# Splitting three raw weight blocks ahead of the first sum in the seven-product pairs of a float32 encoder

## The chip, the core and the metric

The kernel runs on one NeuronCore of a Trainium2 chip. The metric is the device time of one execution in microseconds. The reported time is the median of three runs; one further execution was profiled, and its span runs from the first to the last instruction of the program.

The engines are named as the profile names them: PE is TensorE (matmuls), PEld its weight loads, DVE is VectorE, ACT is ScalarE, POOL is GpSimd and SP is SyncE, which here issues the weight DMAs. Every engine works through its own queue strictly in order.

## The reference

The reference is a two-layer encoder trunk in float32, with 256 tokens of width 2048. Each layer has a token mixer (a chunked spatial gate in layer 0, grouped-query attention in layer 1), a cross-attention into 256 memory tokens, and a dense SwiGLU feed-forward block:

```python
def swiglu(h, w_gate_up, w_down):
    gate, up = jnp.split(h @ w_gate_up, 2, axis=-1)
    return (jax.nn.silu(gate) * up) @ w_down

for l in range(DEPTH):                      # 2
    h = rms_norm(x, g_mix[l])
    ...                                     # token mixer, memory attention
    x = x + jnp.concatenate([tok_out, mem_out], axis=-1) @ w_out[l]
    x = x + swiglu(rms_norm(x, g_ffn[l]), w_gate_up[l], w_down[l])
```

`w_gate_up` is 2048 x 11264 and `w_down` 5632 x 2048 for each layer. The change touches the feed-forward block alone.

## The kernel before

**Three matmuls for one.** Every float32 operand is split in two: a high part `hi`, its copy in the rounded type fp32r, and a low part `lo`, the operand less its high part. A float32 product is then three fp32r matmuls (`matmul3`, lines 198 to 200): L198 is weight-high times activation-high, L199 weight-high times activation-low, L200 weight-low times activation-high. So L198 and L199 need only `whi`, the high part of the weights, and L200 needs `wlo`. The splits of weights are made on chip: ACT makes `whi` by a copy (L254), and DVE makes `wlo` by a subtraction (L255).

**Units.** The feed-forward block works in pairs of 512 output columns (class `Pair`): a gate and an up block of the same 512 features, or two column blocks of `w_down`. A pair goes through its rows in 8 units (6 in the last third of `w_down`); a unit is 256 rows, two DMAs of 512 KB into one tile `raw` with four blocks of 128x512. In the tile's order they are called w01, w00, w10 and w11. There are four `raw` buffers, so the DMA of a unit can start when the unit four places earlier has no reader left.

**Eights and sevens.** An ordinary unit, an eight, makes eight block products (`eight`, 24 matmuls of 512 columns): one split of all four blocks serves them. Some units make seven products instead, after Winograd's form of Strassen's algorithm (`seven`, 21 matmuls). They need four sums of weight blocks. `prepare` makes them on DVE: t1 = w01 + w00 in place of w01 in the `raw` tile (L347, called the first sum below), and t2, t3 and t4 in a tile `T` (L348 to L350). `prepare` of the next unit is called ahead of the products of the present one. There are 82 sevens: three in each gate/up pair (two in the first pair of a layer), standing as first, third and fifth unit, and 18 in the down pairs.

**Split tiles.** `halves` writes one `whi` and one `wlo` tile. An eight takes one such pair of tiles. A seven takes two: its first holds t1, w00, w10 and w11 (one ACT copy and one DVE subtraction of 128x2048), its second t2, t3 and t4 (128x1536 each). There are three buffers of either kind, so a copy into a split tile starts when PE has made its last matmul with the split tile three places earlier.

**Products and banks.** Products 1, 5, 6 and 7 add up in banks of the tag `m`, products 2, 3, 4 and 8 in banks of the tag `acc`. Product 1 uses w00, 2 uses w10, 3 uses w11; 5, 6, 7 and 4 use t1, t2, t3 and t4. In the first unit of a pair 1, 5, 6 and 7 are written ahead of 2, 3 and 4; in later sevens 1, 2 and 3 stand first.

**Order.** The order in each engine's queue isn't the order of the code. The framework's scheduler sets it when the program is built, by its own estimate of what is ready. It places single matmuls of different units, and DVE's sums, subtractions and bank sums, among one another.

Of the kernel before, what the change touches and what calls it, by code (L numbers as in the profile page):

```python
# [10 lines left out]
F32 = mybir.dt.float32  # L11
F32R = mybir.dt.float32r
AF = mybir.ActivationFunctionType
ALU = mybir.AluOpType
AX = mybir.AxisListType

P = 128
# [10 lines left out]
NB = 512  # L28
# [3 lines left out]
KC4 = 4  # L32
# [4 lines left out]
KC3 = 3  # L37


class Parts:  # L40
# [8 lines left out]
    def get(self, kc, t):  # L49
        return self.ap[kc, t]  # L50
# [3 lines left out]
def encoder(ctx: ExitStack, tc: tile.TileContext, x, mem, g_mix, g_ffn, w_in_a, g_v_a, w_spatial, b_spatial,  # L54
            w_in_b, g_q_b, g_k_b, g_mem, w_mem_kv, g_mq, g_mk, w_out, w_gate_up, w_down, rope_c, rope_s, out):
    nc = tc.nc
# [4 lines left out]
    wp = ctx.enter_context(tc.tile_pool(name="wp", bufs=W_TILES))  # L61
# [9 lines left out]
    def nm(s):  # L71
        uid[0] += 1
        return f"{s}_{uid[0]}"
# [25 lines left out]
    def tick():  # L99
        clock[0] += 1  # L100
        run_due(clock[0])
# [146 lines left out]
    def halves(raw, n, step=KC4):  # L248

        hi = wp.tile([P, KC4, NB], F32R, tag="whi", name=nm("whi"))[:, :n]  # L250
        lo = wp.tile([P, KC4, NB], F32R, tag="wlo", name=nm("wlo"))[:, :n]
        for c in range(0, n, step):
            cut = slice(c, min(c + step, n))
            nc.scalar.copy(hi[:, cut], raw[:, cut])  # L254
            nc.vector.tensor_tensor(lo[:, cut], raw[:, cut], hi[:, cut].bitcast(F32), ALU.subtract)  # L255
        return [(hi[:, c, :], lo[:, c, :]) for c in range(n)]

    class Linear:


# [49 lines left out]
    class Pair:  # L310
# [54 lines left out]
            matmul3(self.bank[name], a, b, self.part[name] == 1, self.part[name] == self.of.get(name, self.most))  # L365

        def seven(self, i, raw, T):
            t1, w00, w10, w11 = halves(raw, KC4)
            t2, t3, t4 = halves(T, KC3)
            get, (q5, s2, q7, q3) = self.parts.get, self.sums[i]  # L370
            k0, k1 = 2 * i, 2 * i + 1
            inner = [(1, get(k0, 0), w00), (5, q5, t1), (6, s2, t2), (7, q7, t3)]
            outer = [(2, get(k1, 0), w10), (3, q3, w11), (4, get(k1, 1), t4)]
            if self.bank:
                inner, outer = inner[:1] + outer[:2], inner[1:] + outer[2:]
            for some in (inner, outer):
                for name, a, b in some:
                    self.add(name, a, b)
                tick()
# [225 lines left out]
    for l in range(DEPTH):  # L605
# [105 lines left out]
        else:  # L711
# [12 lines left out]
            for c in range(3):  # L724
                acc = linear(hT, w, c * NB)
                attend(head_norm(acc, norm.r, ghead["q"], True), (7, 8, 11, 13), lambda: own["k"], lambda: own["v"],
                       lambda h, c=c: (4 * c + h) // 3, 4 * c, cat)
# [32 lines left out]
        for chunk in (range(0, 4), range(4, 8), range(8, 11)):  # L760
# [20 lines left out]
            for f, g in pairs.items():  # L781
                g.run(pairs.get(f + 1))
                for t in range(NT):
                    a = kp.tile([P, NB], F32, tag="sg", name=nm("sg"), bufs=2)
# [63 lines left out]
```

## Time and profile before

| | |
|---|---|
| median of 3 runs | 2045.56 us (2045.43 to 2046.12) |
| profiled execution, its own time | 2045.77 us |
| its span, first to last instruction | 2044.0 us |
| PE busy | 2028.7 us, 99% of the span |
| DVE busy | 1604.7 us, 79% |
| ACT busy | 1095.1 us, 54% |
| feed-forward block of layer 0 | about 339 to 1029 us of the span |
| feed-forward block of layer 1 | about 1355 to 2040 us |

A row of a group names the line, the engine, the operation, what is written and read, the shapes and the count; then the busy time and the mean duration in ns; then the engine's idle time ahead of these instructions and what ended it. A row of a timeline gives start, duration, engine, line, operation and tiles; idle time ahead of it stands in brackets. Consecutive 512-column matmuls start 0.227 us apart while PE is supplied, and each is shown as 0.39 us long because they overlap.

### The profile page before, as it was taken

What the parts mean: (1) busy time and instruction counts of PE and PEld (TensorE: products, weight loads), DVE (VectorE), ACT (ScalarE), POOL (GpSimd) and SP (SyncE); (2) the same over time, 40 slices, a digit from 0 to 9 for tenths busy, and PEclk for the clock granted to TensorE, in tenths of its full rate; (3) what the DMA queues carried; (4) which work ended last, traced back from release to release, by engine and by line L of the source; (5) the groups of instructions that cost most, each with busy time, mean ns of one, the idle gap of its engine ahead of it and who ended that gap; (6) DMA issues with size and microseconds to landing.
All of it is one profiled execution on the core that took longest, in us unless ns stands there. A gap on an engine that the chain in (4) does not pass through costs nothing.

```text
span 2044.0 us, 24691 instructions
## 1 busy us (share of the span) xinstructions
PE 2028.7 (99%) x9298; PEld 1679.5 (82%) x9298; DVE 1604.7 (79%) x1862; ACT 1095.1 (54%) x1389; POOL 49.1 (2%) x80
## 2 busy tenths in 40 slices
PE   8999999999999999999999999999999999999999
PEld 6888888888888888888888888888888888888887
DVE  5575557998888988887666876589979899798976
ACT  7765455455444554445556665555544455444552
POOL 2010000000000000000010100000000000000000
PEclk9999999999999999999999999999999999999999
DMA  9754554655656556566556434655666555665554
GB/s 330 249 177 159 187 187 148 227 168 203 208 190 220 169 201 208 200 215 209 188 190 212 157 124 142 206 179 172 205 206 211 200 176 195 206 216 196 181 197 138
DMA packets 202432, 396.08 MB, mean 194 GB/s; under 512 B 11068, under 2 KB 11432, under 8 KB 202312
## 3 DMA queue, kind: packets, MB, share of 16 engines
q1 hardware_dynamic: 198800, 385.79, 56.4%
q0 software_dynamic: 2048, 6.42, 1.0%
q10 hardware_dynamic: 1464, 2.28, 0.3%
q8 instruction: 73, 1.20, 0.2%
q14 instruction: 47, 0.39, 0.1%
HBM read 390.26 MB, written 4.19 MB: 193 GB/s over the span
## 4 chain that ended last, share of the span: by engine, by line
PE 94%; DVE 3%; DMA 1%; issue 1%; ACT 1%; SPq 0%; DVEq 0%; ACTq 0%
PE acc L200 27%; PE acc L198 27%; PE acc L199 27%; PE m L200 4%; PE m L198 4%; PE m L199 4%; PE m L204 2%; DVE wlo L255 1%; DMA raw<-in_w_gate_up 1%; ACT whi L254 0%; PE m L500 0%; DMA x<-in_x 0%; DMA raw<-in_w_down 0%; PE m L643 0%; DVE x L413 0%
## 5 line engine op out<-in xcount | busy, mean ns | idle before, releaser
L255 DVE TENSOR_TENSOR wlo<-raw,whi 128x2048 fp32r<-128x2048 f32 (+2 forms) x465 | 836.4, 1822 | 227.0 <-ACT whi L254 224.8
L254 ACT CAST whi<-raw 128x2048 fp32r<-128x2048 f32 (+2 forms) x465 | 700.9, 1539 | 584.6 <-PE acc L199 513.3
L198 PE MATMUL acc<-whi,h 128*128 128x512 f32 x1440 | 563.6, 392 | 0.8 <-ACT whi L254 0.8
L199 PE MATMUL acc<-whi,h 128*128 128x512 f32 x1440 | 562.6, 391 | 0.0
L200 PE MATMUL acc<-wlo,h 128*128 128x512 f32 x1440 | 523.8, 392 | 1.1 <-DVE wlo L255 1.1
L198 PE MATMUL acc<-whi,a 128*128 128x512 f32 x1062 | 415.4, 392 | 0.6 <-DVE a L431 0.6
L199 PE MATMUL acc<-whi,a 128*128 128x512 f32 x1062 | 414.9, 391 | 0.0
L200 PE MATMUL acc<-wlo,a 128*128 128x512 f32 x1062 | 398.8, 391 | 0.1
L200 PEld LDWEIGHTS acc<-wlo,h 128*128 128x128 f32 x1440 | 270.6, 188 | 56.9 <-DVE wlo L255 1.9
L198 PEld LDWEIGHTS acc<-whi,h 128*128 128x128 f32 x1440 | 270.7, 188 | 55.4 <-ACT whi L254 1.2
L199 PEld LDWEIGHTS acc<-whi,h 128*128 128x128 f32 x1440 | 270.6, 188 | 55.0
L200 PEld LDWEIGHTS acc<-wlo,a 128*128 128x128 f32 x1062 | 199.7, 188 | 41.5 <-DVE wlo L255 0.5
L198 PEld LDWEIGHTS acc<-whi,a 128*128 128x128 f32 x1062 | 199.9, 188 | 41.3 <-DVE a L431 0.8
L199 PEld LDWEIGHTS acc<-whi,a 128*128 128x128 f32 x1062 | 199.9, 188 | 40.5
L254 ACT CAST whi<-T 128x1536 fp32r<-128x1536 f32 x82 | 121.4, 1481 | 143.3 <-PE acc L199 104.1
L255 DVE TENSOR_TENSOR wlo<-T,whi 128x1536 fp32r<-128x1536 f32 x82 | 143.5, 1750 | 38.8 <-ACT whi L254 38.8
L198 PE MATMUL m<-whi,a 128*128 128x512 f32 x264 | 104.2, 395 | 0.7 <-ACT whi L254 0.7
L199 PE MATMUL m<-whi,a 128*128 128x512 f32 x264 | 102.8, 390 | 0.0
L347 DVE TENSOR_TENSOR raw<-raw 128x512 f32<-128x512 f32 x82 | 56.1, 684 | 56.4 <-DMA raw<-in_w_gate_up 54.3
L200 PE MATMUL m<-wlo,a 128*128 128x512 f32 x264 | 89.6, 389 | 0.0
L192 ACT CAST a<-m 128x512 fp32r<-128x512 f32 x80 | 46.3, 586 | 50.7 <-PE m L204 32.6
L193 DVE TENSOR_TENSOR a<-m,a 128x512 fp32r<-128x512 f32 x80 | 54.0, 683 | 17.5 <-ACT a L192 17.5
(126 smaller groups left out, 1469.0 us busy)
## 6 DMA issues: line engine op xcount, KB each, us to landing
raw<-in_w_gate_up SPq DMA_DIRECT2D x352, 512.0 KB, 4.7
raw<-in_w_down SPq DMA_DIRECT2D x176, 512.0 KB, 5.2
raw<-in_w_out SPq DMA_DIRECT2D x32, 1024.0 KB, 5.1
raw<-in_w_in_a SPq DMA_DIRECT2D x24, 1024.0 KB, 5.3
raw<-in_w_in_b SPq DMA_DIRECT2D x24, 1024.0 KB, 5.2
raw<-in_w_mem_kv SPq DMA_DIRECT2D x16, 1024.0 KB, 5.2
raw<-in_w_in_a SPq DMA_DIRECT2D x7, 512.0 KB, 6.1
x<-in_x SPq DMA_DIRECT2D x8, 256.0 KB, 5.7
```

Source lines behind the costliest of these rows:

```text
L192: nc.scalar.copy(hi, src)
L193: nc.vector.tensor_tensor(lo, src, hi.bitcast(F32), ALU.subtract)
L198: nc.tensor.matmul(out, lhsT=a[0], rhs=b[0], start=start, stop=False)
L199: nc.tensor.matmul(out, lhsT=a[1], rhs=b[0], start=False, stop=False)
L200: nc.tensor.matmul(out, lhsT=a[0], rhs=b[1], start=False, stop=stop)
L204: nc.tensor.transpose(dst[:, c * P:(c + 1) * P], src[:, c * P:(c + 1) * P], ident)
L254: nc.scalar.copy(hi[:, cut], raw[:, cut])
L255: nc.vector.tensor_tensor(lo[:, cut], raw[:, cut], hi[:, cut].bitcast(F32), ALU.subtract)
L347: nc.vector.tensor_tensor(raw[:, 0], raw[:, 0], raw[:, 1], ALU.add)
```

## The change

`seven` splits in another grouping. Its first split tile now holds the three blocks that come from memory as they are: w00, w10 and w11, by one ACT copy and one DVE subtraction of 128x1536. Its second split tile holds t1 to t4, by a new function `halves_of`: a copy and a subtraction of 128x512 for t1 out of `raw`, then a copy and a subtraction of 128x1536 for t2, t3 and t4 out of `T`. The number of tiles, buffers, DMAs and matmuls is what it was; each seven has one more ACT copy and one more DVE subtraction.

```diff
+    def halves_of(pieces):
+
+        hi = wp.tile([P, KC4, NB], F32R, tag="whi", name=nm("whi"))
+        lo = wp.tile([P, KC4, NB], F32R, tag="wlo", name=nm("wlo"))
+        c = 0
+        for a in pieces:
+            cut = slice(c, c + a.shape[1])
+            nc.scalar.copy(hi[:, cut], a)
+            nc.vector.tensor_tensor(lo[:, cut], a, hi[:, cut].bitcast(F32), ALU.subtract)
+            c = cut.stop
+        return [(hi[:, i, :], lo[:, i, :]) for i in range(c)]
+
...
         def seven(self, i, raw, T):
-            t1, w00, w10, w11 = halves(raw, KC4)
-            t2, t3, t4 = halves(T, KC3)
+            w00, w10, w11 = halves(raw[:, 1:], KC3)
+            t1, t2, t3, t4 = halves_of((raw[:, 0:1], T))
```

The scheduler orders the queues anew. Three places of that order matter below. In the rows the numbers are those of single buffers; they differ between the two programs, and lines from 259 on are 12 higher in the changed one (L347 becomes L359, L193 stays).

**Place 1, DVE early in the feed-forward block of layer 0.** `raw_3076` (now `raw_3080`) is the first unit of the second pair; `wlo_3012` (now `wlo_3014`) belongs to the second split tile of a seven of the first pair, and `wlo_3049` (now `wlo_3053`) to the eight behind it. Before:

```order
L347 TENSOR_TENSOR raw_3076<-raw_3076 128x512
L306 TENSOR_TENSOR a_2923<-a_2919,a_2923 128x128
L348 TENSOR_TENSOR T_3079<-raw_3076 128x512
L349 TENSOR_TENSOR T_3079<-T_3079,raw_3076 128x512
L350 TENSOR_TENSOR T_3079<-T_3079,raw_3076 128x512
L255 TENSOR_TENSOR wlo_3012<-T_2971,whi_3011 128x1536
L193 TENSOR_TENSOR a_2929<-a_2923,a_2928 128x512
L255 TENSOR_TENSOR wlo_3049<-raw_3004,whi_3048 128x2048
```

After:

```order
L359 TENSOR_TENSOR raw_3080<-raw_3080 128x512
L360 TENSOR_TENSOR T_3083<-raw_3080 128x512
L193 TENSOR_TENSOR a_2929<-a_2923,a_2928 128x512
L361 TENSOR_TENSOR T_3083<-T_3083,raw_3080 128x512
L362 TENSOR_TENSOR T_3083<-T_3083,raw_3080 128x512
L266 TENSOR_TENSOR wlo_3014<-raw_2970,whi_3013 128x512
L266 TENSOR_TENSOR wlo_3014<-T_2973,whi_3013 128x1536
L255 TENSOR_TENSOR wlo_3053<-raw_3006,whi_3052 128x2048
```

Between the first sum and the subtraction of the eight one subtraction of 128x512 has come in, and the 128x128 row L306 has moved ahead of the sum.

**Place 2, PE at the second seven of a later gate/up pair.** `whi_3849` and `whi_3853` (now `whi_3867` and `whi_3871`) are that seven's first and second split tile, `wlo_3818` (now `wlo_3836`) belongs to the eight ahead of it. Before:

```order
L198 MATMUL m_3781<-whi_3849,h_2265 128x512
L199 MATMUL m_3781<-whi_3849,h_2266 128x512
L198 MATMUL m_3785<-whi_3849,a_2879 128x512
L199 MATMUL m_3785<-whi_3849,a_2880 128x512
L198 MATMUL m_3789<-whi_3853,a_2879 128x512
L199 MATMUL m_3789<-whi_3853,a_2880 128x512
L198 MATMUL m_3793<-whi_3853,a_2879 128x512
L199 MATMUL m_3793<-whi_3853,a_2880 128x512
L200 MATMUL acc_3797<-wlo_3818,h_2431 128x512
```

After:

```order
L198 MATMUL m_3799<-whi_3867,h_2265 128x512
L199 MATMUL m_3799<-whi_3867,h_2266 128x512
L198 MATMUL m_3803<-whi_3871,a_2879 128x512
L199 MATMUL m_3803<-whi_3871,a_2880 128x512
L198 MATMUL m_3807<-whi_3871,a_2879 128x512
L199 MATMUL m_3807<-whi_3871,a_2880 128x512
L198 MATMUL m_3811<-whi_3871,a_2879 128x512
L199 MATMUL m_3811<-whi_3871,a_2880 128x512
L200 MATMUL acc_3815<-wlo_3836,h_2431 128x512
```

The products stand in the same order (1, 5, 6, 7); product 5, with t1, now reads the second split tile, and products 6 and 7, with t2 and t3, stand where they stood.

**Place 3, DVE at the start of the second down pair of layer 0.** `raw_4344` (now `raw_4370`) is that pair's first unit, a seven; `wlo_4241` and `wlo_4245` (now `wlo_4265` and `wlo_4269`) are those of a seven of the first down pair, and `wlo_4282` (now `wlo_4308`) belongs to the eight behind that. Before:

```order
L193 TENSOR_TENSOR a_4162<-m_4156,a_4161 128x512
L255 TENSOR_TENSOR wlo_4241<-raw_4201,whi_4240 128x2048
L255 TENSOR_TENSOR wlo_4245<-T_4204,whi_4244 128x1536
L347 TENSOR_TENSOR raw_4344<-raw_4344 128x512
L255 TENSOR_TENSOR wlo_4282<-raw_4237,whi_4281 128x2048
L405 TENSOR_TENSOR x_0_89<-x_0_89,e_4269 128x512
```

After:

```order
L193 TENSOR_TENSOR a_4184<-m_4178,a_4183 128x512
L255 TENSOR_TENSOR wlo_4265<-raw_4225,whi_4264 128x1536
L266 TENSOR_TENSOR wlo_4269<-raw_4225,whi_4268 128x512
L266 TENSOR_TENSOR wlo_4269<-T_4228,whi_4268 128x1536
L255 TENSOR_TENSOR wlo_4308<-raw_4261,whi_4307 128x2048
L359 TENSOR_TENSOR raw_4370<-raw_4370 128x512
L255 TENSOR_TENSOR wlo_4341<-raw_4304,whi_4340 128x2048
```

The first sum of the new pair's first seven has moved behind the eight's subtraction, and the last reader of the old seven's `raw` tile is now a subtraction into its second split tile.

## Prediction

> **What bounds the kernel now.** I read the page's totals first, then the chain that ended last.
>
> ```profile
> span 2044.0 us, 24691 instructions
> PE 2028.7 (99%) x9298; PEld 1679.5 (82%) x9298; DVE 1604.7 (79%) x1862; ACT 1095.1 (54%) x1389; POOL 49.1 (2%) x80
> PE 94%; DVE 3%; DMA 1%; issue 1%; ACT 1%; SPq 0%; DVEq 0%; ACTq 0%
> ```
>
> PE is busy in all but 15.3 us of the span (2044.0 - 2028.7), and the chain lies on PE for 94%. The change leaves PE's work alone, so it can save no more than waits of PE, and cost no more than the waits it adds. The next question is which waits the change touches: who waits for the first sum (L347), and what the copies into the split tiles (L254) wait for, from the view of waits and that of the line L347.
>
> ```profile
> ACT whi L254 <- PE acc L199: 617.4, 225, 7.4
> DVE raw L347 <- DMA raw<-in_w_gate_up: 54.3, 20, 4.9
> ...
> who waited for it (us, times):
> ...
>   ACT whi L254: 1.1, 1
> ```
>
> In 82 sevens ACT waited for the first sum once, for 1.1 us. It waited 617.4 us for PE to give back a split tile. The splits run ahead as far as three buffers let them, and the sums are made earlier still. DVE itself waits 54.3 us for weights to land ahead of first sums.
>
> Then I looked for the stretches of the feed-forward blocks in which PE does stand still, with two others beside them.
>
> ```profile
> core 0: us, PE busy (x) PEld busy (x) DVE busy (x) ACT busy (x) POOL busy (x), PEclk, DMA share, GB/s
> 330.00:380.00 50.00, 48.55 (x211) 39.13 (x210) 45.49 (x58) 26.95 (x27) 0.95 (x1) 1.00 0.49 163
> 380.00:430.00 50.00, 50.00 (x226) 41.42 (x225) 45.10 (x44) 27.48 (x22) 0.00 (x0) 1.00 0.61 208
> 355.00:358.00 3.00, 1.86 (x9) 1.23 (x8) 3.00 (x2) 2.28 (x3) 0.00 (x0) 1.00 0.00 0
> 371.00:376.00 5.00, 4.69 (x20) 3.24 (x19) 5.00 (x5) 3.56 (x3) 0.00 (x0) 1.00 0.33 82
> 519.00:525.00 6.00, 5.88 (x26) 4.57 (x25) 4.66 (x6) 4.40 (x4) 0.00 (x0) 1.00 0.05 11
> 798.00:802.00 4.00, 3.81 (x17) 2.71 (x16) 4.00 (x3) 2.27 (x2) 0.00 (x0) 1.00 0.27 68
> 1385.00:1390.00 5.00, 4.71 (x20) 3.27 (x19) 5.00 (x6) 3.13 (x2) 0.00 (x0) 1.00 0.27 59
> 1811.00:1815.00 4.00, 3.82 (x17) 2.70 (x16) 4.00 (x3) 2.40 (x2) 0.00 (x0) 1.00 0.25 57
> ```
>
> From 380 to 430 us, an ordinary stretch of sevens and eights, PE is busy without a gap, and DVE has a tenth of its time left. The six short stretches hold PE waits of 1.14, 0.31, 0.12, 0.19, 0.29 and 0.18 us, 2.23 us together. All lie where a feed-forward block or a pair begins. Counted by the starts of matmuls instead of their modelled ends they come to about twice that, since a wait also thins out the matmuls around it. So 2 to 4.5 us is what the change could win.
>
> **The change part by part.** The prices of the instructions, from the groups kept apart by shape:
>
> ```profile
> L254 ACT CAST whi<-raw 128x2048 fp32r<-128x2048 f32 x264 | 500.0, 1914 | 482.2 <-PE acc L199 426.6 <-issue 39.0 <-DVE T L348 4.4
> L254 ACT CAST whi<-T 128x1536 fp32r<-128x1536 f32 x82 | 121.4, 1481 | 143.3 <-PE acc L199 104.1 <-PE m L199 31.0 <-DVE T L350 7.1
> L192 ACT CAST a<-a 128x512 fp32r<-128x512 f32 x15 | 9.3, 618 | 1.3 <-DVE a L306 1.3
> L255 DVE TENSOR_TENSOR wlo<-raw,whi 128x2048 fp32r<-128x2048 f32 x264 | 599.4, 2285 | 105.7 <-ACT whi L254 104.9
> L255 DVE TENSOR_TENSOR wlo<-T,whi 128x1536 fp32r<-128x1536 f32 x82 | 143.5, 1750 | 38.8 <-ACT whi L254 38.8
> L347 DVE TENSOR_TENSOR raw<-raw 128x512 f32<-128x512 f32 x82 | 56.1, 684 | 56.4 <-DMA raw<-in_w_gate_up 54.3 <-DMA raw<-in_w_down 2.1
> ```
>
> A seven's splits cost DVE 2.285 + 1.750 = 4.035 us before, and 1.750 + 0.684 + 1.750 = 4.184 us after: 0.15 us more, 12.2 us over 82 sevens. On ACT it is 1.914 + 1.481 = 3.395 us against 1.481 + 0.618 + 1.481 = 3.580 us, 0.19 us more, less a further overlap of about 0.1 us.
>
> Term A, the wait for the first sum that goes: between -1.1 us and 0. I take 0, because the copies around it wait for PE's buffers anyway.
>
> The added work on DVE costs nothing while PE's queue is supplied (380 to 430 us: 4.9 us of cover in 50, against some 0.5 us that three or four sevens add). It costs what it lasts where DVE is late already.
>
> Term B, place 1 of the order:
>
> ```profile
> 349.83 0.69 DVE L347 TENSOR_TENSOR raw<-raw 128x512 f32<-128x512 f32 x1 [2.19 <-DMA raw<-in_w_gate_up]
> ...
> 354.84 4.49 DVE L255 TENSOR_TENSOR wlo<-raw,whi 128x2048 fp32r<-128x2048 f32 x2
> ...
> 357.18 0.50 PE L200 MATMUL acc<-wlo,h 128*128 128x512 f32 x1 [1.14 <-DVE wlo L255]
> ```
>
> DVE starts at the landing of a DMA and works without a gap until PE gets the eight's low half. Between the two the order now has one subtraction of 128x512 more, 0.68 us, and one small row fewer: +0.6 us. Bounds 0 (the landing comes earlier) and 1.3 us (two sevens' additions count). The landing itself waits for an eight's buffer, which the change doesn't touch.
>
> Term C, place 2, the second seven of a gate/up pair:
>
> ```profile
> 456.26 1.91 ACT L254 CAST whi<-raw 128x2048 fp32r<-128x2048 f32 x1 [0.93 <-ACT sg L785]
> 458.07 1.48 ACT L254 CAST whi<-T 128x1536 fp32r<-128x1536 f32 x1
> ...
> 457.37 0.39 PE L199 MATMUL acc<-whi,h 128*128 128x512 f32 x1
> ...
> 458.73 0.39 PE L198 MATMUL m<-whi,h 128*128 128x512 f32 x1
> ...
> 459.64 0.47 PE L198 MATMUL m<-whi,a 128*128 128x512 f32 x1
> ```
>
> The second split tile is t2 to t4 here; ACT finishes it at 459.55, and PE needs it at 459.64. Its buffer comes free when the matmul of 457.37 has ended, about 457.85. After the change t1 is copied into it first: 457.85 + 0.62 + 1.48 - 0.10 (the copies overlap: 458.17 against 458.07) = 459.85, or 0.2 us too late. The first split tile, three blocks now, is ready earlier, which doesn't help, since PE comes to it at 458.73 in either program. The same order with so little room stands at four such sevens, and at two more (in the stretches of 371 and 1385 us) ACT comes late anyway and about 0.1 us is added. Sum 4 x 0.2 + 2 x 0.1 = +1.0 us. Bounds 0 and 6 x 0.52 = 3.1 us, the whole added copy.
>
> Term D, place 3, a second down pair's start:
>
> ```profile
> 511.16 2.29 DVE L255 TENSOR_TENSOR wlo<-raw,whi 128x2048 fp32r<-128x2048 f32 x1 [0.26 <-ACT whi L254]
> ...
> 520.62 0.69 DVE L347 TENSOR_TENSOR raw<-raw 128x512 f32<-128x512 f32 x1 [1.34 <-DMA raw<-in_w_down]
> ...
> 543.12 4.48 DVE L255 TENSOR_TENSOR wlo<-raw,whi 128x2048 fp32r<-128x2048 f32 x2
> ...
> 516.01 1.48 ACT L254 CAST whi<-T 128x1536 fp32r<-128x1536 f32 x1 [4.88 <-PE m L199]
> ...
> 523.07 0.39 PE L199 MATMUL acc<-whi,a 128*128 128x512 f32 x1
> 523.58 0.50 PE L200 MATMUL acc<-wlo,a 128*128 128x512 f32 x1
> ...
> 545.76 0.39 PE L200 MATMUL acc<-wlo,a 128*128 128x512 f32 x1
> ...
> raw<-in_w_down SPq DMA_DIRECT2D x176, 512.0 KB, 5.2
> ```
>
> The raw tile of the seven at 511 us had its last reader end at 513.45. That reader's successor is now the subtraction for t1, and it needs the second split tile, free at 516.01: 516.01 + 0.62 + 0.68 = 517.3. So the DMA of the new pair's first unit starts 3.85 us later on SP's queue, and its sum, 520.62 before, can start between about 522.9 (517.3, the median 5.2, and a little for the second of the two DMAs) and 524.5 (520.62 + 3.85). Behind that waiting sum stand the next eight's subtraction and the sums of the banks, for which PE waits in turn. Ahead of it DVE now makes the eight's low half, so PE's wait at 523.58 goes: 0.4 us with the thinned matmuls behind it. From the sum DVE worked without a gap to the low half of the new pair's second unit, an eight: the first of the two of 543.12, done at 545.40 and read at 545.76. That run of 24.78 us loses the eight's 2.2 and one sum of 0.6 that moved behind it, and gains 0.15: 22.1 us. It ends between 545.0 and 546.6; PE comes at 545.4 if its earlier wait is gone. That is 0 to 1.2 us of new wait. Four second down pairs have this shape. I take 0.2 us each, near the low end, since the table's DMA share of 0.05 at 519 to 525 us shows an idle queue: 4 x 0.2 - 0.4 = +0.4 us. Bounds: -0.4 and 4 x 1.2 - 0.4 = +4.4; the waits near 799 and 1812 us may change by 0.4 us either way.
>
> The sum is 0 + 0.6 + 1.0 + 0.4 = +2.0 us. On the profiled execution's own 2045.77 us (span 2044.0 and 1.8 around it) that is 2047.8; it lies 0.2 above the median of the runs, so I predict 2047.6 us. The ends are -1.1 - 0.4 - 0.8 = -2.3 and +1.3 + 3.1 + 4.4 + 0.8 = +9.6: 2043.3 and 2055.2.
>
> **The rivals.**
> - Nothing of this reaches PE, 2045.6 us. For it: the 617.4 us that ACT waits on PE, which can swallow tenths of a microsecond anywhere; against it: the 0.09 us of room in term C. The change would then do what it says to the sums, but no one waits for them.
> - Faster: the waits where pairs begin all go, because three blocks no longer stand behind sums on a busy DVE. 2045.6 - 2.2 = 2043.3, by starts of matmuls 2041.1 us. For it: five of the six stretches have DVE at 100%. Against: in those of 371, 798, 1385 and 1811 us PE's last wait ends with a copy into the second tile, which the change makes later.
> - Slower: raw buffers come back too late in the four second down pairs. It decides once the new unit lands later than 523.3 (545.4 - 22.1). With 1.2 us at each, and B and C as above: 2045.6 + 0.6 + 1.0 + 4.4 = 2051.6 us. A long wait would cost more than itself:
>
> ```profile
> PE m L500 <- DVE a L490: 2.6, 1, 2.6
> ...
> 1205.00:1216.00 11.00, 7.79 (x33) 6.13 (x33) 9.63 (x29) 6.66 (x28) 1.83 (x2) 0.84 0.28 95
> ```
>
>   after PE's 2.6 us wait in layer 1's attention the granted clock averaged 0.84 over 11 us, some 1.8 us lost. [...]
> - Slower: DVE becomes the bound. All 12.2 us come through: 2057.8 us. Against it: 10% of idle time in the densest stretch.
>
> **How the numbers follow.** A measurement of this kernel can tell about 0.2%, 4.1 us, from no change: 2041.5 and 2049.7. My forecast, a loss too small to tell, 0.52 at 2047.6; nothing at all 0.20; all waits gone 0.08; late buffers 0.15; DVE the bound 0.05. Faster takes half of the third, 0.04. Slower takes the last two and a little of the forecast, 0.22. The rest, 0.74, is no change. The range 2043.2 to 2053.0 leaves out the end of the third and the last case.
>
> **What would show it.** PE's busy time stays at 2028.7 within 1 us, and ACT still waits for PE in hundreds of places. DVE's busy time rises by about 12 us. PE's wait near 357 us grows to about 1.7 us, that near 523 goes, and a wait of some 0.2 us on a copy of 128x1536 appears near 459.6. If DVE waits for a down weight beyond 523.3, late buffers are at work. I am wrong if PE's waits in the feed-forward blocks fall below 1 us, or rise by more than 4 us.

## The result and the profile after

The change makes the kernel slightly slower: 2051.32 us, median of 8 runs (2049.02 to 2053.56), against 2046.51 us for the kernel before, also 8 runs (2044.51 to 2048.58). The ratio is 1.0025 with a 95% interval of 1.0016 to 1.0034, so about 4.8 us are lost. I had predicted 2047.6 us, 2.0 us more than before, and a loss too small to tell. The loss is small, but it can be told: the interval does not contain 1.

The profiled execution of the changed kernel took 2052.54 us. Its page begins so (totals, then the shares of the chain that ended last):

```profile
span 2050.7 us, 24848 instructions
PE 2032.9 (99%) x9298; PEld 1680.3 (82%) x9298; DVE 1611.7 (79%) x1944; ACT 1104.0 (54%) x1471; POOL 49.2 (2%) x80
PE 88%; DVE 6%; issue 3%; DMA 2%; ACT 1%; SPq 0%; DVEq 0%; ACTq 0%
```

PE's matmuls are as many as before (9298), but the chain now lies on DVE for 6% of the span instead of 3%. DVE's busy time rose by 7.0 us (1604.7 to 1611.7) and ACT's by 8.9 (1095.1 to 1104.0). The view of waits shows for whom PE stood still:

```profile
PE m L512 <- DVE a L502: 2.6, 1, 2.6
PE acc L198 <- DVE x L425: 1.8, 5, 0.4
...
PE m L198 <- ACT whi L265: 1.3, 2, 0.6
PE acc L200 <- DVE wlo L255: 1.1, 2, 0.8
```

The second row is new. L425 (L413 before) is the line of the bank sums at the end of a down pair: it adds a bank of the tag `acc` to `x` and so gives the bank back. PE waited for it five times. The third row is the copy of t1 or of T into the new second split tile. All PE waits shown in the feed-forward blocks come to 4.8 us, against 2.2 before.

The waits are shown with modelled ends of matmuls, so I measured the loss by starts. Both traces have 9298 matmuls; the n-th of one is set against the n-th of the other, and the difference of their start times says how far the changed kernel is behind. What this difference grows by in a stretch is what the stretch lost. The stretches are named by the times of the kernel before.

| stretch | lost, us | the prediction's term |
|---|---|---|
| 450-470, 700-730, 1465-1490, 1720-1750: four second sevens of gate/up pairs | 1.23 | C: 4 x 0.2 |
| 1355-1374: layer 1's counterpart of place 1 | 0.53 | none |
| 1374-1400: the seven behind it | 0.23 | C: 0.1 |
| 470-560, 730-810, 1490-1580, 1750-1830: the down pairs, all of it from the second pair's first sum on | 2.96 | D: 0.4 |
| 340-365: place 1 | 0.19 | B: 0.6 |
| all other stretches of the feed-forward blocks | -0.01 | C: 0.1 at 365-380, else 0 |
| 1200-1230: attention of layer 1 | 1.43 | none |
| 0-340: everything ahead of the first feed-forward block | 0.16 | none |

Together 6.7 us, the difference of the two spans. The long stretches in between, 560 to 700 us for one, lost 0.01 us: there the added instructions cost nothing.

The largest entry is the second down pairs. DVE in the first of them, in the view of the timeline:

```profile
517.87 0.69 DVE L266 TENSOR_TENSOR wlo<-raw,whi 128x512 fp32r<-128x512 f32 x1 [3.75 <-PE m L200]
...
524.15 0.69 DVE L359 TENSOR_TENSOR raw<-raw 128x512 f32<-128x512 f32 x1 [0.90 <-DMA raw<-in_w_down]
...
543.32 0.68 DVE L425 TENSOR_TENSOR x<-acc,x 128x512 f32<-128x512 f32 x1
543.92 2.27 DVE L255 TENSOR_TENSOR wlo<-raw,whi 128x2048 fp32r<-128x2048 f32 x1
546.12 0.68 DVE L425 TENSOR_TENSOR x<-acc,x 128x512 f32<-128x512 f32 x1
546.72 1.74 DVE L255 TENSOR_TENSOR wlo<-raw,whi 128x1536 fp32r<-128x1536 f32 x1
548.39 0.68 DVE L266 TENSOR_TENSOR wlo<-raw,whi 128x512 fp32r<-128x512 f32 x1
548.99 1.75 DVE L266 TENSOR_TENSOR wlo<-T,whi 128x1536 fp32r<-128x1536 f32 x1
```

The subtraction of t1 at 517.87 is the last reader of the raw tile. The first sum of the new pair, whose weights go into that tile, then stood in front of DVE's queue for 0.90 us with the weights not there, until 524.15. The subtraction behind it stood as long, until 524.76, though the copy that it reads had ended at 522.74 (the second of two of ACT from 519.03 on, 3.71 us together). From there DVE had no gap. The bank sum that ended at 544.00 let PE go on at 544.05. PE in the same place, and at the second pair of this kind, where it happened twice:

```profile
543.28 0.40 PE L199 MATMUL acc<-whi,a 128*128 128x512 f32 x1
544.05 0.50 PE L198 MATMUL acc<-whi,a 128*128 128x512 f32 x1 [0.37 <-DVE x L425]
...
546.25 0.50 PE L200 MATMUL acc<-wlo,a 128*128 128x512 f32 x1
...
796.99 0.50 PE L198 MATMUL acc<-whi,a 128*128 128x512 f32 x1 [0.31 <-DVE x L425]
...
799.99 0.50 PE L198 MATMUL acc<-whi,a 128*128 128x512 f32 x1 [0.38 <-DVE x L425]
```

The low half of the eight, for which I had expected PE to wait, was ready at 546.19 (543.92 + 2.27) and read at 546.25.

### The profile page after: what moved, and what is told of

Its sections match the earlier page's. It is cut to its first block, busy times and chain, and to the rows that moved or that the text cites. A ratio compares the mean times of both kernels' runs of the same rounds, so it can differ in the third digit from the quotient of the medians.

```text
span 2050.7 us, 24848 instructions
## 1 busy us (share of the span) xinstructions
PE 2032.9 (99%) x9298; PEld 1680.3 (82%) x9298; DVE 1611.7 (79%) x1944; ACT 1104.0 (54%) x1471; POOL 49.2 (2%) x80
## 4 chain that ended last, share of the span: by engine, by line
PE 88%; DVE 6%; issue 3%; DMA 2%; ACT 1%; SPq 0%; DVEq 0%; ACTq 0%
PE acc L200 25%; PE acc L198 25%; PE acc L199 25%; PE m L198 3%; PE m L199 3%; PE m L200 3%; PE m L204 2%; DVE wlo L255 1%; DMA raw<-in_w_down 1%; DVE wlo L266 1%; DMA raw<-in_w_gate_up 1%; ACT whi L265 1%; DVE x L417 0%; DVE T L361 0%; DVE T L360 0%
## 5 line engine op out<-in xcount | busy, mean ns | idle before, releaser
L254 ACT CAST whi<-raw 128x2048 fp32r<-128x2048 f32 (+3 forms) x465 | 665.8, 1462 | 557.3 <-PE acc L199 469.4
L255 DVE TENSOR_TENSOR wlo<-raw,whi 128x2048 fp32r<-128x2048 f32 (+3 forms) x465 | 793.0, 1728 | 215.3 <-ACT whi L254 212.8
L266 DVE TENSOR_TENSOR wlo<-T,whi 128x1536 fp32r<-128x1536 f32 x82 | 143.5, 1750 | 6.6 <-ACT whi L265 6.5
L265 ACT CAST whi<-raw 128x512 fp32r<-128x512 f32 x82 | 50.9, 621 | 153.2 <-PE acc L199 152.6
L359 DVE TENSOR_TENSOR raw<-raw 128x512 f32<-128x512 f32 x82 | 56.2, 685 | 61.5 <-DMA raw<-in_w_gate_up 56.7
L266 DVE TENSOR_TENSOR wlo<-raw,whi 128x512 fp32r<-128x512 f32 x82 | 56.1, 684 | 37.6 <-ACT whi L265 22.6
```

Source lines behind the costliest of these rows:

```text
L265: nc.scalar.copy(hi[:, cut], a)
L266: nc.vector.tensor_tensor(lo[:, cut], a, hi[:, cut].bitcast(F32), ALU.subtract)
L359: nc.vector.tensor_tensor(raw[:, 0], raw[:, 0], raw[:, 1], ALU.add)
```

## The experiments

After this comparison I held **theory 1**: the loss is made in the second down pairs, because t1's subtraction gives the raw buffer back late. **Theory 2**, its rival: the added copies and subtractions themselves cost the time, spread over all 82 sevens. Each kernel below was run in five rounds beside the kernel before. I give the difference of the medians, and in brackets the interval of the ratio turned into us.

**The new splits in the gate and up sevens alone, and in the down sevens alone.**

```diff
 def seven(self, i, raw, T):
+    if self.into:                        # a down pair
+        t1, w00, w10, w11 = halves(raw, KC4)
+        t2, t3, t4 = halves(T, KC3)
+    else:
         w00, w10, w11 = halves(raw[:, 1:], KC3)
         t1, t2, t3, t4 = halves_of((raw[:, 0:1], T))
```

> The new order of splits in the 64 gate and up sevens alone; the 18 down sevens are split as before. Theory 1 (the loss is made where a second down pair begins, because the raw buffer is given back late): what is left is the copy of the first sum ahead of the second split tile, about 0.27 us at each of four second sevens and some 0.1 us at two more places, so +1.0 to +1.5 us against the kernel before, and PE's waits on the bank sums stay as they were. Theory 2 (the loss is the added copies and subtractions themselves): 64 of 82 parts of 4.8 us, +3.7 us.

Measured: +4.3 us (+2.7 to +6.3), ratio 1.0022 (1.0013 to 1.0031).

The other way round (the two branches exchanged):

> The new order of splits in the 18 down sevens alone; the 64 gate and up sevens are split as before. Theory 1: nearly the whole loss stands here, +3 to +3.8 us against the kernel before, as waits of PE on the bank sums near 544, 797, 1558 and 1812 us, with the first sum of each of these pairs waiting for its DMA beyond 523.3 us. Theory 2: 18 of 82 parts of 4.8 us, +1.1 us.

Measured: +0.1 us (-1.8 to +1.6), ratio 0.9999 (0.9991 to 1.0008).

Theory 1 has fallen as an account of the whole. Nearly all of the loss comes with the gate and up sevens, and the down sevens alone cost nothing that can be measured, though two of the waits on bank sums that theory 1 expected are there (0.38 us at 798.36 and 0.31 us at 1813.21). The totals look like theory 2, but the trace of the first kernel doesn't: by starts of matmuls it lost 1.26 us at the four second sevens, 0.86 at the start of layer 1's block and 1.03 at the second down pairs, and 0.02 in all other stretches of the feed-forward blocks. Yet its down sevens are split as before. What changed there is PE's queue. The seven in question is the third unit of a second down pair; in the kernel before the scheduler had put 20 matmuls between its t1 and the first use of its second split tile, here none:

```
before                                          gate and up sevens alone
L199 MATMUL m_724_4399<-whi_736_4463            L199 MATMUL m_724_4421<-whi_736_4485
L200 MATMUL acc_727_4411<-wlo_733_4432          L198 MATMUL m_725_4425<-whi_738_4489
...                                             ...
L199 MATMUL acc_728_4415<-whi_736_4463
L198 MATMUL m_725_4403<-whi_738_4467
```

(`whi_738` is that second split tile, `wlo_733` the low half of the eight ahead.) In the trace of the gate and up sevens alone, PE and ACT read:

```profile
545.45 1.48 ACT L254 CAST whi<-T 128x1536 fp32r<-128x1536 f32 x1
...
546.40 0.40 PE L199 MATMUL m<-whi,a 128*128 128x512 f32 x1
546.98 0.50 PE L198 MATMUL m<-whi,a 128*128 128x512 f32 x1 [0.18 <-ACT whi L254]
```

The copy ended at 546.93 and PE went on at 546.98, 0.58 after the matmul ahead instead of 0.23. The kernel before asked for the same tile only here, with no wait:

```profile
544.58 1.48 ACT L254 CAST whi<-T 128x1536 fp32r<-128x1536 f32 x1
...
550.32 0.39 PE L198 MATMUL m<-whi,a 128*128 128x512 f32 x1
```

Of its four second down pairs the kernel before has this later order in the first and third, and the early order, with a wait of the same kind, in the second and fourth:

```profile
800.32 0.50 PE L198 MATMUL m<-whi,a 128*128 128x512 f32 x1 [0.19 <-ACT whi L254]
```

(the fourth has it at 1813.45 us). With the new gate and up splits all four have the early order: two more waits of 0.48 us by starts.

**t1 by its own instructions, but in the first split tile.**

```diff
+def halves_by(raw):                       # one split tile, two copies, two subtractions
+    for cut in (slice(1, 4), slice(0, 1)):
+        nc.scalar.copy(hi[:, cut], raw[:, cut])
+        nc.vector.tensor_tensor(lo[:, cut], raw[:, cut], hi[:, cut].bitcast(F32), ALU.subtract)
...
 def seven(self, i, raw, T):
-    w00, w10, w11 = halves(raw[:, 1:], KC3)
-    t1, t2, t3, t4 = halves_of((raw[:, 0:1], T))
+    t1, w00, w10, w11 = halves_by(raw)
+    t2, t3, t4 = halves(T, KC3)
```

> The three raw blocks are split first, as in the change, and the first sum by its own copy and subtraction, but into the fourth block of the same split tile; the second split tile holds t2, t3 and t4 as before. The count of instructions and their sizes are those of the change; only the raw buffer is given back with the first split tile again. Theory 1: the loss goes, 0 to +0.7 us against the kernel before, and the first sum of a second down pair waits no longer than before (1.34 us at 520.62). Theory 2: the instructions are all there, so +4 to +5 us as with the change.

Measured: +1.7 us (-0.2 to +3.3), ratio 1.0007 (0.9999 to 1.0016). It lies between the two theories. By starts, 0.44 us were lost at the second sevens and 1.18 at the second down pairs, where PE's queue has the early order again. So the count of instructions doesn't fix the time, against theory 2, and not all is gained back by an early raw buffer, against theory 1.

**The raw buffer given back later still.** The down sevens alone, with t1 behind T:

```diff
-    t1, t2, t3, t4 = halves_of((raw[:, 0:1], T))
+    t2, t3, t4, t1 = halves_of((T, raw[:, 0:1]))
```

> As the run with the down sevens alone, but the second split tile takes t2 to t4 first and the first sum last, so that a raw buffer is given back some 1.5 to 1.8 us later still. Theory 1: the waits at the four second down pairs grow by up to that much each: 1 to 6 us above the run with the down sevens alone, +4 to +10 us against the kernel before. Theory 2: the same instructions in the same number, so the same time as the run with the down sevens alone.

Measured: -0.9 us (-2.7 to +1.0), ratio 0.9996 (0.9987 to 1.0005). Both theories expected a loss. PE doesn't wait once in the second down pairs of this kernel. DVE shows why:

```profile
519.97 0.69 DVE L266 TENSOR_TENSOR wlo<-raw,whi 128x512 fp32r<-128x512 f32 x1
520.63 2.29 DVE L255 TENSOR_TENSOR wlo<-raw,whi 128x2048 fp32r<-128x2048 f32 x1
...
526.84 2.28 DVE L255 TENSOR_TENSOR wlo<-raw,whi 128x2048 fp32r<-128x2048 f32 x1
529.04 0.68 DVE L359 TENSOR_TENSOR raw<-raw 128x512 f32<-128x512 f32 x1
```

The raw tile came free at 520.66, 2.1 us later than in the change (518.56, the end of the row at 517.87). But its next first sum now stands behind three of the eights' subtractions, not behind one, at 529.04, and doesn't wait: its DMA has landed by then. The work that PE needs was done meanwhile.

This gave **theory 3**: what costs time is the place in an in-order queue that the scheduler gives to an instruction whose data aren't there yet. In DVE's queue that is the waiting first sum ahead of the eights' subtractions, in PE's the second split tile's products ahead of the eight's low ones. Beside it stands the simple part, t1's copy ahead of T's in the second split tile. No run changes the order alone, since each moves it by another split or another position of a unit. So theory 3 rests on what the traces of all these kernels show together.

**The whole change, with t1 behind T in the down sevens.**

```diff
+    if self.into:
+        t2, t3, t4, t1 = halves_of((T, raw[:, 0:1]))
+    else:
         t1, t2, t3, t4 = halves_of((raw[:, 0:1], T))
```

> The whole change, except that the second split tile of the 18 down sevens takes t2 to t4 first and the first sum last. In this program the first sum of a second down pair stands in DVE's queue behind three of the eights' subtractions (behind one in the change), and the bank sums stand ahead of the low half of the eight. Theory 3 (what costs time at the second down pairs is the place in DVE's or PE's queue that the scheduler gives to an instruction whose data are not there yet): the waits on the bank sums are gone at all four pairs although each raw buffer is given back later still, and no copy is waited for there, as in the run with the late order in the down sevens alone; +2 to +3 us against the kernel before, all of it from the gate and up sevens. Theory 1 (late raw buffers): +5 us or more. Theory 2 (the added instructions): +4.8 us as with the change.

Measured: +2.0 us (0.0 to +3.5), ratio 1.0009 (1.0000 to 1.0017). No wait on a bank sum is left in PE's list, whose rows for the feed-forward blocks begin so:

```profile
PE m L198 <- ACT whi L265: 1.5, 3, 0.7
PE acc L200 <- DVE wlo L255: 1.0, 2, 0.8
```

One wait on a copy was left in the second down pairs, which I had not expected:

```profile
800.09 0.50 PE L198 MATMUL m<-whi,a 128*128 128x512 f32 x1 [0.23 <-ACT whi L265]
```

The second down pairs went from +2.96 to -0.61 us by starts, while the second sevens kept their 1.25.

**Gate and up sevens with t1 in the first split tile.** As `halves_by` above, in the gate and up pairs only.

> The 64 gate and up sevens split their three raw blocks first and then the first sum, by instructions of its own, into the fourth block of the same split tile; their second split tile holds t2, t3 and t4 as before, and the 18 down sevens are split as before. So it has the instructions of the run with the gate and up sevens alone, without the first sum's copy ahead of t2 to t4. In PE's queue the products of the third unit's second split tile stand behind the low products of the eight at all four second down pairs; in the kernel before they do so at two of them, in the run with the gate and up sevens alone at none. Theory 3: about +0.1 us at each of the four second sevens, some +0.2 us at the start of a feed-forward block, and -0.4 us at the two pairs whose order got better: -0.5 to +1 us. Theory 2: as the run with the gate and up sevens alone, +3.7 to +4.3 us.

Measured: -0.3 us (-2.3 to +1.4), ratio 0.9998 (0.9989 to 1.0007). It makes the same copies and subtractions as the gate and up sevens alone and takes 4.6 us less, by the two differences (4.3 and -0.3), or 3.6 us less by the starts (3.2 and -0.4). That is the end of theory 2. By starts the second down pairs gained 1.01 us, with PE's queue in the later order at all four, and the second sevens lost 0.44 instead of 1.26. The second seven at 459 us, in this kernel:

```profile
456.16 2.00 ACT L263 CAST whi<-raw 128x1536 fp32r<-128x1536 f32 x2 [1.30 <-PE acc L199]
458.06 1.49 ACT L254 CAST whi<-T 128x1536 fp32r<-128x1536 f32 x1
...
459.60 0.50 PE L198 MATMUL m<-whi,a 128*128 128x512 f32 x1
```

and in the change:

```profile
455.93 1.49 ACT L254 CAST whi<-raw 128x1536 fp32r<-128x1536 f32 x1 [1.22 <-issue]
457.32 0.72 ACT L797 ACTIVATE sg<-e,s 128x512 f32<-128x512 f32 x1
458.21 0.62 ACT L265 CAST whi<-raw 128x512 fp32r<-128x512 f32 x1 [0.17 <-PE acc L199]
458.74 1.48 ACT L265 CAST whi<-T 128x1536 fp32r<-128x1536 f32 x1
...
459.77 0.39 PE L199 MATMUL m<-whi,a 128*128 128x512 f32 x1
460.26 0.50 PE L198 MATMUL m<-whi,a 128*128 128x512 f32 x1
```

In the change the buffer came free at 458.21; t1's copy took 0.53 of start-to-start time, T's ended at 460.22, and PE, which stood ready at 460.00 (459.77 + 0.23), went on at 460.26. This is term C as it was worked out.

**The sevens of a first down pair moved.** At positions 1 and 3 of the units instead of 2 and 4, the second pair's first unit takes the raw buffer of an eight, not of a seven. Tried on the kernel before and on the change:

```diff
-    order.insert(2 * n + (0 if jj and not last else 2), i)
+    order.insert(2 * n + (0 if jj and not last else 2 if last else 1), i)
```

> The kernel before with the sevens of a first down pair at positions 1 and 3 of its units instead of 2 and 4, so that the first unit of the second pair takes the raw buffer of an eight. Theory 3: PE's order at the second down pairs is the better one throughout, so the two waits of about 0.4 us near 800 and 1813 us go: 0 to -1 us against the kernel before. It is the counterpart of the next run.

Measured: +0.7 us (-1.2 to +2.5), ratio 1.0003 (0.9994 to 1.0012).

> The change with the same move of the sevens of a first down pair. Theory 1 and theory 3 agree here: no raw buffer that the new pair waits for is held by a first sum, and PE never waits for a bank sum at the second down pairs, so what is left above the run before it is the gate and up part, about 1.2 us at the second sevens and 0.8 us at the start of the second layer's block, +2 to +3 us. Theory 2 (added instructions): +4.8 us, the whole difference between the change and the kernel before.

Measured: +1.3 us (-0.2 to +3.5), ratio 1.0008 (0.9999 to 1.0017). Both expectations missed their size in part. The second down pairs did as expected: PE waited for no bank sum there, and by starts, from the second pair's first sum on, they gained 1.74 us in either run. But the first run had new waits in each first down pair, 0.53 us by starts, such as this one, with ACT's copies ahead of it:

```profile
503.52 1.91 ACT L254 CAST whi<-raw 128x2048 fp32r<-128x2048 f32 x1 [5.39 <-PE acc L199]
...
505.80 1.91 ACT L254 CAST whi<-raw 128x2048 fp32r<-128x2048 f32 x1
...
507.77 0.50 PE L198 MATMUL m<-whi,a 128*128 128x512 f32 x1 [0.19 <-ACT whi L254]
```

With the new splits they are not there (0.00 us in all four first pairs, against 2.11). So the two runs differ by only 0.6 us. Here the new splits pay for part of what they cost elsewhere.

That pointed to a combination: the moved sevens, and the new splits in the down sevens alone.

> The sevens of a first down pair at positions 1 and 3 of its units, the change's splits in the 18 down sevens, and the gate and up sevens split as before. Theory 3: no wait at the second down pairs (-1.6 us against the kernel before, as in both runs with the moved sevens), none in the first down pairs either (the run with the moved sevens alone had one of 0.5 us in each, the run with the change and the moved sevens none), and nothing lost in the gate and up sevens: -0.5 to -2.5 us against the kernel before, about as much as such a measurement can tell. Theory 2 (added instructions): 18 of 82 parts of 4.8 us more than the run with the moved sevens alone, +1.8 us.

Measured: -1.9 us (-3.1 to +0.4), ratio 0.9993 (0.9985 to 1.0002), 2043.76 us. Of PE's waits in the feed-forward blocks only these are left:

```profile
PE acc L200 <- DVE wlo L255: 0.4, 1, 0.4
PE m L198 <- ACT whi L254: 0.4, 2, 0.2
```

The same with t1 in the first split tile:

> The same, but the first sum of a down seven is split, after the three raw blocks, into the fourth block of the first split tile, so the second split tile is not held up. Theory 3: as the run before it, -0.5 to -2.5 us against the kernel before. In PE's queue the third unit of a second pair here stands a little earlier; should PE wait for its second split tile near 545 us, that would cost up to 0.5 us at each pair again. Theory 2: as the run before it.

Measured: -1.3 us (-2.5 to +1.2), ratio 0.9997 (0.9988 to 1.0006). The first of the two is the best kernel of this study. It is better than the change beyond its interval; against the kernel before the interval still holds 1, so a gain is likely and not shown.

**All runs in one table.** By starts of matmuls against the kernel before, in us. The rest holds place 1. The sum leaves out what lies ahead of 340 us and the attention stretch of 1200 to 1230 us, for a reason given below.

| kernel | second sevens | start of layer 1's block | down pairs | rest | sum | measured |
|---|---|---|---|---|---|---|
| the change | 1.23 | 0.76 | 2.96 | 0.18 | 5.1 | +4.8 |
| gate and up sevens alone | 1.26 | 0.86 | 1.03 | 0.00 | 3.2 | +4.3 |
| down sevens alone | -0.04 | -0.04 | 0.41 | 1.20 | 1.5 | +0.1 |
| down sevens alone, t1 behind T | -0.04 | 0.32 | -1.09 | -0.29 | -1.1 | -0.9 |
| all sevens, t1 in the first tile | 0.44 | 0.21 | 1.18 | -0.27 | 1.6 | +1.7 |
| the change, t1 behind T in the down sevens | 1.25 | 0.99 | -0.61 | -0.19 | 1.4 | +2.0 |
| gate and up sevens, t1 in the first tile | 0.44 | 0.27 | -1.01 | -0.07 | -0.4 | -0.3 |
| before, moved sevens | -0.02 | 0.01 | 0.36 | 0.09 | 0.4 | +0.7 |
| the change, moved sevens | 1.24 | 0.73 | -1.75 | 1.28 | 1.5 | +1.3 |
| down sevens alone, moved | -0.04 | 0.31 | -1.74 | -0.82 | -2.3 | -1.9 |
| the same, t1 in the first tile | 0.00 | -0.03 | -1.19 | -0.05 | -1.3 | -1.3 |

The sums, each from a single profiled execution, follow the measured differences of medians to about half a microsecond, but for two rows. In the third the profiled execution was the slowest of its 11 runs (2048.14 us against a median of 2045.91), and 1.5 us of it were lost behind two late landings of gate/up weights; for the first of them DVE waited 5.79 us, until 603.84.

The second row falls short by 1.1 us, inside the interval of its measurement. Part of this is likely the clock in the attention stretch, which the sums leave out and the medians hold (see the last section). With the gate and up sevens alone eight of ten executions had a mean granted clock of 0.998, the kernel before beside it in seven of 32. At a like clock the two differ by 3.7 us on average (0.998) and by 3.1 (0.999, two executions only), beside 3.2 by starts.

## Why the prediction was right or wrong

**What bounds the kernel** was right. PE still sets the end, and the change lost at most 0.01 us in a stretch where its queue was supplied: there the added instructions cost nothing by themselves. The sign that I gave for it failed: PE's busy time rose from 2028.7 to 2032.9 us, not within 1 us, with the same matmuls. A matmul beside a wait is shown longer (0.50 us at 544.05 instead of 0.39), so a part of each loss stands in the busy time.

**The prices of the added instructions** were too high on DVE and somewhat low on ACT. The busy times rose by 7.0 us and 8.9, where I had 12.2 and about 7 (82 x 0.09). I had added up durations, but in a queue without gaps an instruction costs the distance from its start to the next one's. In the rows from 546.72 on, a subtraction of 128x1536 takes 1.67 us of it and one of 128x512 0.60; the two of 128x2048 at 543.12 in the kernel before take 2.20 each (547.52 - 543.12 = 4.40). A seven's added DVE time is then 1.67 + 0.60 - 2.20 = 0.07 us, 5.7 over 82 sevens, not 0.15.

**Term A**, nothing gained by the first sum's wait that goes: no stretch of the change shows a gain from it. The 2.11 us of the first down pairs with moved sevens are not such a gain: in the rows above ACT waited for PE, and from 470 to 515 us all six waits of that kernel's copies, 19.6 us, were for PE.

**Term B**, +0.6 us at place 1: the mechanism was right, at 0.4 us, and an earlier landing, by luck, hid half of it. The stretch of 340 to 365 us lost 0.19. DVE and PE there:

```profile
349.75 0.69 DVE L359 TENSOR_TENSOR raw<-raw 128x512 f32<-128x512 f32 x1 [2.18 <-DMA raw<-in_w_gate_up]
...
355.17 4.48 DVE L255 TENSOR_TENSOR wlo<-raw,whi 128x2048 fp32r<-128x2048 f32 x2
...
353.63 0.50 PE L200 MATMUL m<-wlo,a 128*128 128x512 f32 x1 [0.18 <-DVE wlo L266]
...
357.50 0.50 PE L200 MATMUL acc<-wlo,h 128*128 128x512 f32 x1 [0.79 <-DVE wlo L255]
```

From the first sum to the eight's subtractions DVE took 5.42 us (355.17 - 349.75), against 5.01 before (354.84 - 349.83), so 0.41 more. But the landing came 0.21 us earlier, set against PE: 349.75 instead of 349.83, with the kernel 0.13 us behind there. 0.41 - 0.21 is the 0.19 lost, within rounding. PE's last wait became shorter, not 1.7 us long, because PE now waits for the second split tile's low half as well, at 353.63: by starts it lost 0.5 us there, and 0.3 of it came back at the last wait.

Over the eleven kernels this stretch lay between -0.71 and +0.63 us. With the shift of the landing taken out, the four with t1 in the second split tile of the gate and up sevens lost 0.39 to 0.45 us, with 5.41 or 5.42 us on DVE. The other seven lost 0.00 to 0.05, with 5.01 or 5.02. Two of these seven also split t1 by instructions of its own in the gate and up sevens, but in the first split tile.

I had priced one place where there are two. At the start of layer 1's block DVE works through the same sequence:

```profile
1367.29 0.69 DVE L359 TENSOR_TENSOR raw<-raw 128x512 f32<-128x512 f32 x1 [1.13 <-DMA raw<-in_w_gate_up]
...
1372.71 4.48 DVE L255 TENSOR_TENSOR wlo<-raw,whi 128x2048 fp32r<-128x2048 f32 x2
```

Again 5.42 us, against 5.01 before (1368.41 - 1363.40), and here the landing came 0.14 us later: 0.53 us lost. The same four kernels lost 0.39 us in it with the landing taken out, the others -0.01 to 0.12. B was thus +0.72 us.

**Term C** was right in its mechanism, with 0.31 us at each of the four second sevens where I had 0.2. Its two further places were sized at 0.1 each. The one in layer 0 (365 to 380 us) lost 0.03. The one in layer 1 lost 0.23, behind the wait that belongs to B:

```profile
1375.04 0.50 PE L200 MATMUL acc<-wlo,h 128*128 128x512 f32 x1 [0.29 <-DVE wlo L255]
...
1392.68 0.50 PE L198 MATMUL m<-whi,a 128*128 128x512 f32 x1 [0.65 <-ACT whi L265]
```

C was thus +1.49 us, not +1.0.

**Term D** is where the size went wrong: 0.4 us predicted, 2.96 measured, within the bound of 4.4 that I had set aside as unlikely. Step by step: the wait at 523.58 went, as predicted (-0.41 us from 515 to 531). The first sum started at 524.15, and the changed kernel ran 0.65 us behind just ahead of that time, so at 523.5 on the clock of before: inside 522.9 to 524.5, and just beyond the 523.3 that I gave as the point where late buffers begin to decide. DVE's run from there to the low half took 22.04 us (546.19 - 524.15), predicted 22.1. What failed is the step from there to PE. I let PE wait for the low half alone. It waited for the bank sums ahead of that half, which I had named as queued behind the first sum but had not priced. And I took one place for four. The second and fourth pair have another order in PE's queue than the first already in the kernel before; I had given them "0.4 us either way", and they lost 0.95 and 0.57.

The rival of late buffers (2051.6 us) came nearest in time, in part by luck: it has 4.4 us for D where 2.96 were measured, and 1.6 for B and C where it was 2.2. Its waits are all in the trace. But the runs showed that a late buffer is not enough for it. The down sevens alone have a late buffer and lost 0.41 us in the second pairs; a still later one gained 1.09. The 2.96 us are those 0.41, 1.03 us that the gate and up sevens bring by the changed order of PE's queue, and 1.5 us that appear only when both come together. The two that put the waiting first sum elsewhere, or take its lateness away (t1 behind T, moved sevens), both end the waits on bank sums. That the scheduler reorders places whose own code isn't touched had no term in my sum, and no rival.

**Nothing of this reaches PE** and **all waits go** are excluded by the interval. **DVE the bound** is excluded by the stretches that lost nothing.

The whole sum: +2.0 predicted, as 0 + 0.6 + 1.0 + 0.4. By the trace it is 0 + 0.72 + 1.49 + 2.96 = 5.2, 5.1 with all other stretches, and 4.8 measured. So the forecast had the right way and, for B and C, the right mechanisms. That the time still lies in the range is owed to the upper bounds that I gave to C and D, not to the sum.

## What to carry to other kernels

Where a scheduler sets the order of in-order queues, an edit moves instructions at places that it doesn't touch, and the place of one waiting instruction can matter more than its lateness: here a late raw buffer lost 0.41 us in the second down pairs, and one given back later still, with another place for the first sum that waits for it, gained 1.09. So compare the new order at every instance of a place, not at one, and price everything that is queued between the wait and the instruction that the bounding engine needs. Where that wait is for a DMA, take the shift of its landing out first: it hid half of what place 1 cost (0.21 of 0.41 us). To see where microseconds go in a kernel that is 99% bound by one engine, set the n-th instruction of that engine in one trace against the n-th in the other: the stretches that lose show at once, and here their sums matched the timed runs to about half a microsecond in nine of eleven kernels.

## What the runs showed of the hardware

In every kernel of this case PE waits 2.63 us once, in the attention of layer 1, and in ten of the twelve profiled executions 0.58 us once more behind it. The cost of that place differed from one profiled execution to the next. The stretch of 1200 to 1225 us (behind the engines' busy times, the third number from the end is the granted clock), first in the kernel before, then in the change, then in the kernel with the gate and up sevens' t1 in the first tile:

```profile
1200.00:1225.00 25.00, 21.79 (x119) 18.54 (x118) 16.58 (x40) 14.82 (x45) 1.83 (x2) 0.93 0.25 85
```

```profile
1200.00:1225.00 25.00, 21.79 (x105) 18.07 (x104) 14.93 (x37) 13.31 (x44) 1.83 (x2) 0.86 0.25 85
```

```profile
1200.00:1225.00 25.00, 21.79 (x130) 18.88 (x129) 17.40 (x41) 15.66 (x47) 1.84 (x2) 1.00 0.29 95
```

The granted clock was 0.93, 0.86 and 1.00: a loss of 1.75, 3.5 and 0 us of full clock (25 x 0.07, 25 x 0.14, 0). The other profiled executions show the same three values and no other: of the twelve, seven have 0.93, four 0.86 and one 1.00. By starts of matmuls the stretch of 1200 to 1230 us was 1.43 us longer in the change than before, and 1.47 shorter in the third.

Narrower stretches show how the loss is made up. In the kernel before the clock reads 0.50 from 1209.7 to 1213.0 us, and 1.00 from 1206.0 to 1208.4 and from 1213.1 to 1217.0; in the change it reads 0.50 from 1211.5 to 1218.2. In the third kernel it reads 1.00 from 1204 to 1228. In the stretch at 0.50 in the kernel before, matmuls of 512 columns started 0.43 us apart (1210.38, 1210.81, 1211.23), behind it 0.23 (1213.45, 1213.69, 1213.92). So the loss was made in these 3.3 and 6.7 us at a clock of 0.50: 1.65 and 3.35 us of the 1.75 and 3.5. The wait of 2.63 us stands in all twelve executions, the lower clock in eleven. With the gate and up sevens alone, one of the two without the second wait, PE was busy for 3.60 us of the stretch of 1204 to 1208 us, so the wait lasted from about 1207.6 to 1210.2. The clock was 1.00 in that stretch, 0.73 from 1208 to 1212 and 0.50 from 1212 to 1216. By an estimate from these values, with 0.50 from its fall up to 1212, it fell at about 1209.8 (0.27 x 4 / 0.5 = 2.2 us ahead of 1212), within the wait.

The timed runs show it too. Of 33 runs of the kernel before, 22 had a mean clock of 0.999 and took 2045.3 us on average, ten had 0.998 and took 2046.9. Whether the time at which the wait begins has a part in it wasn't tried. The kernels may not be alike in it: with the gate and up sevens alone eight of ten runs had 0.998, with the down sevens alone one of eleven. This clock is why the stretch is left out of the sums above, and one source of the 2 us by which the runs of one kernel differ.
